# Sums of weight blocks by adding DMAs, with the products of neighbouring pairs interleaved

## The chip, the cores and the metric

The kernel runs on one core of one Trainium2 chip. The metric is the device time of one execution, in microseconds (us).

## What is computed

A decoder trunk of two layers on 512 positions of width 1024, batch 1, everything in fp32. A layer has three steps; each adds to x a gated function of a modulated RMS norm of x:

```python
x = x + 0.5 * gate[:, 0] * swiglu(ada(x, 0), ffn_w1[l, 0], ffn_w2[l, 0])
x = x + gate[:, 1] * mixer(ada(x, 1), w_in[l], ..., w_out[l])
x = x + 0.5 * gate[:, 2] * swiglu(ada(x, 2), ffn_w1[l, 1], ffn_w2[l, 1])
```

`ada(x, i)` is `rmsnorm(x) * (1 + scale_i) + shift_i`; shift, scale and gate are `silu(c) @ w_ada[l] + b_ada[l]`. `swiglu(h)` is `(silu(h @ w1_gate) * (h @ w1_up)) @ w2`, with a hidden width of 2816. The mixer is dilated attention beside a short convolution; the change does not touch it.

## The kernel before, in words

**Number format.** Every fp32 weight block and activation is split into two fp32r parts, hi (an ACT copy) and lo (a DVE subtraction); a product is three matmuls, hi*hi, hi*lo and lo*hi (`halves` L159, `product` L249, `shared_bulk` L255).

**FFN, first matrix.** The 22 hidden tiles of 128 are taken as 11 pairs. A pair's 1024 x 256 part of w1 (gate and up) is four blocks of 128 x 1024, b11, b12, b21 and b22, and the pair is computed with seven products of 2x2 blocks (Winograd's form of Strassen) in place of eight. Products 1, 2 and 4 take the loaded blocks b11, b12, b22. The others take sums of blocks: 5 takes s = b21 + b22, 6 takes s - b11, 7 takes b11 - b21 as combined at L199, 3 takes b12 - (s - b11). Before, all of them are loaded by SP (seven loads of 512 KB for a pair, `load_unit` L173), and DVE makes the four sums (`combine` L185 in `split_unit` L180). One product of a pair is called a unit here: 24 matmuls of 256 columns.

**FFN, second matrix.** After pairs 3, 7 and 10 the finished part of w2 is multiplied ("part" 0, 1, 2): eight steps of 128 output rows, for each a load of 512 or 384 KB, a split, and products over all 512 positions (`Tail.run` L477). Within a pair the products accumulate in three PSUM banks a, b, c of six (L596); `evacuation` (L549) copies bank a with ACT (L564) between the products that share it, adds on DVE (L559), and ends in `hidden` (L566), whose hi and lo parts are what the w2 products read.

**Order.** `_ffn_order` (L83) writes the order of the units out by hand. All weights go through one list of units; `weights` (L219) asks for splits two units ahead of the one in use (AHEAD), and `fetch` (L209) for loads two units ahead of those (LOADED). Loaded blocks lie in six tiles of tag "raw" (L151), the split ones in four tiles each of "whi" and "wlo" (L161). SP issues every load in order, and waits where the next tile is not free.

**Modulation jobs.** The weights w_ada of later steps are reduced by jobs put between the units (`later` L314, `next_job` L307): a job loads a 512 KB block into one of the same six "raw" tiles (`ada_load` L274) and reduces it on DVE (`ada_job` L278, L282). One job follows each pair, three each of the first four pairs of the first FFN (L636), and two each step of a w2 part (L509). The jobs of the second FFN of layer 1 are none: nothing comes after it.

**Ends of steps.** The last part of a step ends in the norm for the next (`Blocks` L423, `change` L526): its first half goes to a tile "hva" of its own, and the seven moving operands of the block products are made from it.

Of the kernel before, what the change touches and what calls it, by code (L numbers as in the profile page):

```python
# [18 lines left out]
D = 1024  # L19
# [83 lines left out]
def trunk(ctx: ExitStack, tc: tile.TileContext, t: dict):  # L103
# [47 lines left out]
    def raw_tile(name="raw"):  # L151
        return wp.tile([128, 1024], F32, name=name, tag="raw", bufs=6)
# [18 lines left out]
    blocks = {}  # L171

    def load_unit(key, src, n):  # L173

        if key[0] != "w1":
            return [load(src, n)]
        b11, b12, b21, b22 = (src[b] for b in range(4))
        return [load(b) for b in {1: (b11,), 2: (b12,), 3: (b12,), 4: (b22,), 5: (b21, b22), 6: (b11,), 7: ()}[key[4]]]

    def split_unit(key, raws, n):  # L180
        if key[0] == "w1":
            pair, which = key[:4], key[4]

            def combine(out, a, b, op):
                nc.vector.tensor_tensor(out=out, in0=a, in1=b, op=op)  # L185

            if which == 5:
                a21, s = raws
                combine(s, a21, s, ALU.add)
                blocks[pair] = [a21, s]  # L190
                raws = [s]
            elif which == 6:
                (a11,), (a21, s) = raws, blocks[pair]
                combine(s, s, a11, ALU.subtract)
                blocks[pair].append(a11)
                raws = [s]
            elif which == 7:
                a21, _, a11 = blocks[pair]
                combine(a11, a11, a21, ALU.subtract)  # L199
                raws = [a11]  # L200
            elif which == 3:
                (a12,), s = raws, blocks.pop(pair)[1]
                combine(a12, a12, s, ALU.subtract)
        return halves(key, raws[0], n)
# [4 lines left out]
    def fetch(upto):  # L209
        for i in range(len(loaded), min(upto + LOADED, len(order))):  # L210
            loaded.append(load_unit(*order[i]))
        for i in range(len(fetched), min(upto, len(order))):
            key, _, n = order[i]
            fetched.append(split_unit(key, loaded[i], n))
            loaded[i] = None
# [58 lines left out]
    def ada_load(w, l, s, m, j):  # L274
        nc.sync.dma_start(w, t["w_ada"][l, (s * 3 + m) * KD + j])
        return w

    def ada_job(l, s, m, j, w=None):  # L278
        raw, _ = mods[l, s]
        if w is None:  # L280
            w = ada_load(raw_tile("ada"), l, s, m, j)
        nc.vector.scalar_tensor_tensor(w, w, 1.0, cb, op0=ALU.mult, op1=ALU.mult,  # L282
                                       accum_out=raw[:, m, j:j + 1])
# [22 lines left out]

    def next_job(n=1):  # L307
# [115 lines left out]
    class Blocks:  # L423

        def __init__(self, l, s, h, pool):
            self.l, self.s, self.h, self.pool = l, s, h, pool

            self.first = [pool.tile([128, KD, 256], F32, name="hva", tag="hva", bufs=1)]

        def half(self, rb, which, k):  # L430

            l, s, h, cols = self.l, self.s, self.h, HALVES[which]
            first = self.first[0]
            a, b = 2 * k, 2 * k + 1
            if which == 0:
                for j, product in ((a, 1), (b, 2)):
                    scaled(first[:, j], l, s, rb, cols, j)
                    shifted(*moving(h, k, product), l, s, first[:, j], j)
# [7 lines left out]
            nc.vector.tensor_tensor(out=v[:, 0], in0=z[:, 0], in1=first[:, a], op=ALU.subtract)  # L446
# [4 lines left out]
            nc.vector.scalar_tensor_tensor(v[:, 3], first[:, b], shift, v[:, 2], op0=ALU.add, op1=ALU.subtract)  # L451
# [9 lines left out]
    class Tail:  # L461
# [15 lines left out]
        def run(self, ks, key, done, pool=None, side_by_side=0):  # L477
# [38 lines left out]
            if not self.last:  # L516
                h = new_h()
                blocks = Blocks(self.nl, self.ns, h, pool) if self.ns != 1 else None
# [97 lines left out]
    def ffn(l, s, h, carried, groups=()):  # L616
# [16 lines left out]
        for group in todo:  # L633
# [10 lines left out]
            room = None  # L644
            if p == len(PARTS) - 1 and s == 2 and l + 1 < DEPTH:
                room = stack.enter_context(tc.tile_pool(name="next", bufs=1))
# [5 lines left out]
    def mixer(l, s, h):  # L652
# [13 lines left out]
        with tc.tile_pool(name="mix", bufs=1) as mp:  # L666
# [142 lines left out]
            for i, k in enumerate((4, 5, 6, 7, 0, 1, 2, 3)):  # L809
                split(yh[i], yl[i], y[k])  # L810
                ks.append((yh[i], yl[i]))
        stack = ExitStack()
# [3 lines left out]
        return tail.run(ks, ("out", l), True, op), stack  # L816


    mod_tile(0, 0)
    stack = ExitStack()  # L820
# [7 lines left out]
    c = sp.tile([1, D], F32, name="c")  # L828
    nc.sync.dma_start(c, t["c"])
# [6 lines left out]
    for half in range(2):  # L836
        ps = acc_bank()
        cols = slice(half * 512, half * 512 + 512)
        nc.tensor.matmul(ps, row, c[:, cols], start=True, stop=True)
# [6 lines left out]
    first = Blocks(0, 0, h, sp)  # L846
    for k in range(KD // 2):
# [3 lines left out]
        for j in (2 * k, 2 * k + 1):  # L851
            for m in range(2):
                ada_job(0, 0, m, j, ada[j][:, m])
# [13 lines left out]
    for l in range(DEPTH):  # L867
        for s in range(3):
            if s == 1:
                stack.close()  # L870
                h, stack = mixer(l, s, h)
# [3 lines left out]
    stack.close()  # L875

# [62 lines left out]
```

## Time and profile before

| what | value |
|---|---|
| time, median of 3 runs | 1958.61 us (1956.05 to 1959.87) |
| time of the profiled execution | 1960.68 us |
| its span, first to last instruction | 1958.9 us |
| TensorE (PE) busy | 1856.1 us, 95% |
| VectorE (DVE) busy | 1551.4 us, 79% |
| ScalarE (ACT) busy | 898.7 us, 46% |
| GpSimd (POOL) busy | 11.9 us, 1% |
| mean granted TensorE clock, of full speed | 0.979 |
| bytes moved | 323.61 MB, 165 GB/s over the span |

The profile is one execution. An engine's busy time is the union of its instructions; matmuls are pipelined, so the time of one is longer than the step from one to the next. "Idle before" a group of instructions is the time in which their engine had nothing running just before them, put down to what ended it. The DMA share is the mean busy share of the core's 16 DMA engines.

### The profile page before, as it was taken

Reading aid. Unit: us, or ns where it says so; the run is one execution under the profiler, and the core shown is the slowest. Engines: PE = TensorE matmul, PEld = TensorE weight load, DVE = VectorE, ACT = ScalarE, POOL = GpSimd, SP = SyncE. Lnnn points to the kernel's source line nnn. Section 1 sums busy time; section 2 is a strip of 40 time slices with the busy share of each in tenths; the row PEclk is TensorE's granted clock in tenths of the full one; section 3 lists DMA queues with packets and bytes.
Section 4 is the critical chain, followed back from the end, with each engine's and each line's share of the span. In section 5 each row is a group of like instructions: output and inputs, shape, how many; then the busy total and the mean of one; then the engine's idle time right before and its main releaser. Section 6 shows DMA issues by size and latency. Waiting matters only on the chain.

```text
span 1958.9 us, 31198 instructions
## 1 busy us (share of the span) xinstructions
PE 1856.1 (95%) x12340; PEld 1718.4 (88%) x12340; DVE 1551.4 (79%) x2593; ACT 898.7 (46%) x1382; POOL 11.9 (1%) x76
## 2 busy tenths in 40 slices
PE   3899999999999899999989999999999998999999
PEld 2888998988988898998978989899898798989898
DVE  8987887897866998884779879788978669858574
ACT  3542442546654453452545425344656535535342
POOL 0000000000000000000000000000000000000000
PEclk9999999999999899999999999999999998999999
DMA  8478667642222167663524676766222123536442
GB/s 325 139 239 277 210 220 239 203 159 70 98 76 97 58 210 263 216 221 114 162 92 162 216 257 205 240 233 208 81 82 94 66 86 121 200 112 198 135 144 83
DMA packets 92613, 323.61 MB, mean 165 GB/s; under 512 B 10161, under 2 KB 11185, under 8 KB 92466
## 3 DMA queue, kind: packets, MB, share of 16 engines
q1 hardware_dynamic: 92466, 321.61, 49.0%
q8 instruction: 97, 1.59, 0.3%
q14 instruction: 50, 0.41, 0.1%
HBM read 319.48 MB, written 2.10 MB: 164 GB/s over the span
## 4 chain that ended last, share of the span: by engine, by line
PE 67%; DVE 17%; DMA 10%; issue 3%; ACT 3%; DVEq 0%; ACTq 0%
PE acc L258 31%; PE acc L251 11%; PE acc L252 10%; PE acc L253 10%; DMA ada<-in_w_ada 8%; DVE wlo L164 4%; DVE ada L282 4%; DVE raw L185 2%; ACT whi L163 2%; DMA raw<-in_w 2%; PE acc L739 1%; DVE h L458 1%; DVE ev L559 1%; PE tp L730 1%; PE tp L759 1%
## 5 line engine op out<-in xcount | busy, mean ns | idle before, releaser
L258 PE MATMUL acc<-h,whi 128*128 128x256 f32 x4928 | 905.6, 287 | 59.7 <-DVE ev L559 25.5
L258 PEld LDWEIGHTS acc<-h,whi 128*128 128x128 f32 x4928 | 776.8, 193 | 67.6 <-issue 26.0
L163 ACT ACTIVATE whi<-raw 128x1024 fp32r<-128x1024 f32 (+1 forms) x476 | 487.2, 1032 | 649.5 <-PE acc L252 298.0
L258 PE MATMUL acc<-h,wlo 128*128 128x256 f32 x2464 | 703.0, 286 | 11.4 <-DVE wlo L164 11.2
L164 DVE TENSOR_TENSOR wlo<-raw,whi 128x1024 fp32r<-128x1024 f32 (+1 forms) x476 | 562.4, 1187 | 90.1 <-ACT whi L163 85.2
L258 PEld LDWEIGHTS acc<-h,wlo 128*128 128x128 f32 x2464 | 475.3, 193 | 14.7 <-DVE wlo L164 14.5
L251 PE MATMUL acc<-hidh,whi 128*128 128x512 f32 (+1 forms) x776 | 286.9, 370 | 0.0
L253 PE MATMUL acc<-hidh,wlo 128*128 128x512 f32 (+1 forms) x776 | 286.7, 370 | 0.0
L252 PE MATMUL acc<-hidl,whi 128*128 128x512 f32 (+1 forms) x776 | 286.7, 369 | 0.0
L185 DVE TENSOR_TENSOR raw<-raw 128x1024 f32<-128x1024 f32 x176 | 214.5, 1221 | 33.6 <-DMA raw<-in_w 32.2
L282 DVE SCALAR_TENSOR_TENSOR ada<-ada,cb 128x1024 f32<-128x1024 f32 x144 | 175.3, 1223 | 59.8 <-DMA ada<-in_w_ada 53.4
L471 DVE SCALAR_TENSOR_TENSOR x<-acc,fin,x 128x512 f32<-128x512 f32 (+1 forms) x130 | 87.6, 675 | 112.1 <-PE acc L253 111.8
L253 PEld LDWEIGHTS acc<-hidh,wlo 128*128 128x128 f32 x776 | 146.3, 188 | 25.0 <-DVE wlo L164 0.2
L252 PEld LDWEIGHTS acc<-hidl,whi 128*128 128x128 f32 x776 | 146.3, 188 | 24.2
L251 PEld LDWEIGHTS acc<-hidh,whi 128*128 128x128 f32 x776 | 146.3, 189 | 24.1
L251 PE MATMUL acc<-h,whi 128*128 128x512 f32 (+1 forms) x368 | 139.8, 380 | 0.0
L252 PE MATMUL acc<-h,whi 128*128 128x512 f32 (+1 forms) x368 | 134.9, 367 | 0.0
L253 PE MATMUL acc<-h,wlo 128*128 128x512 f32 (+1 forms) x368 | 134.7, 366 | 0.0
L564 ACT ACTIVATE ev<-acc 128x512 f32<-128x512 f32 x132 | 76.6, 587 | 58.4 <-PE acc L258 58.4
L559 DVE TENSOR_TENSOR ev<-acc,ev 128x512 f32<-128x512 f32 x132 | 90.5, 687 | 9.5 <-PE acc L258 9.5
L251 PE MATMUL acc<-whi,h 128*128 128x384 f32 x256 | 90.1, 353 | 2.6 <-ACT h L414 2.6
L252 PE MATMUL acc<-wlo,h 128*128 128x384 f32 x256 | 88.0, 344 | 0.0
(99 smaller groups left out, 1669.1 us busy)
## 6 DMA issues: line engine op xcount, KB each, us to landing
raw<-in_w SPq DMA_DIRECT2D x308, 512.0 KB, 3.8
ada<-in_w_ada SPq DMA_DIRECT2D x128, 512.0 KB, 4.4
raw<-in_w2a SPq DMA_DIRECT2D x64, 512.0 KB, 4.2
raw<-in_w2b SPq DMA_DIRECT2D x32, 384.0 KB, 3.1
raw<-in_w_qkv SPq DMA_DIRECT2D x32, 384.0 KB, 3.5
raw<-in_w_gcu SPq DMA_DIRECT2D x24, 512.0 KB, 3.2
ada<-in_w_ada SPq DMA_DIRECT2D x8, 1024.0 KB, 7.3
raw<-in_w_out SPq DMA_DIRECT2D x16, 512.0 KB, 3.2
```

The source lines that it names most:

```text
L163: nc.scalar.activation(hi, raw, AF.Copy)
L164: nc.vector.tensor_tensor(out=lo, in0=raw, in1=hi.bitcast(F32), op=ALU.subtract)
L185: nc.vector.tensor_tensor(out=out, in0=a, in1=b, op=op)
L251: nc.tensor.matmul(out, a[0], b[0], start=first, stop=False)
L252: nc.tensor.matmul(out, a[0], b[1], start=False, stop=False)
L253: nc.tensor.matmul(out, a[1], b[0], start=False, stop=last)
L258: nc.tensor.matmul(out, p, q, start=first and i == 0, stop=i == 2, skip_group_check=True)
L282: nc.vector.scalar_tensor_tensor(w, w, 1.0, cb, op0=ALU.mult, op1=ALU.mult, accum_out=raw[:, m, j:j + 1])
L458: return nc.vector.tensor_tensor(out=lo, in0=v, in1=hi.bitcast(F32), op=ALU.subtract)
L471: nc.vector.scalar_tensor_tensor(x[j][:, cols], ps, gate, x[j][:, cols], op0=ALU.mult, op1=ALU.add)
L559: nc.vector.tensor_tensor(out=v, in0=bank, in1=v, op=ALU.add)
L564: nc.scalar.activation(sums_of[n, i], banks[n, "a"], AF.Copy)
```

## The change

SP loads only b11, b12, b22 and b21 for a pair. The sums are made by four transfers that POOL issues with an addition onto a tile in SBUF: b22 onto the loaded b21 (s); s, from SBUF, onto b11 after ACT has negated it in place (s - b11, in a new tag "sum" with three tiles); b22 onto a "raw" tile in which ACT has written the negated s - b11; b12 onto the negated s - b11. The four DVE sums of a pair go. `_ffn_order` gets a new order from pair 1 on. Job weights get two tiles of their own (tag "ada"), and their load is issued one job ahead and outside the `issue_after` that holds the job's work behind the last `hidden`. To make room, "hva" takes tiles of the tags "hidh" and "hidl" (or a pair of tiles in the pools of the start and of the mixer), c is loaded as two halves into working tiles, and the scratch of the DMAs that POOL issues is set to 4096 bytes.

```diff
@@ _ffn_order
-    order += [[u] for u in ((1, 5), (0, 7), (1, 6), (0, 4), (0, 3), (2, 5), (1, 7), (2, 6), (1, 4), (1, 3), (3, 1),
-                            (2, 7), (3, 5), (2, 4), (2, 3), (3, 6), (3, 2), (3, 7))]
+    order += [[u] for u in ((1, 5), (1, 6), (2, 5), (0, 7), (0, 4), (0, 3), (1, 7), (2, 6), (1, 4), (1, 3))]
     ends = [p0 + n - 1 for p0, n in PARTS]
-    for n in range(3, NP):
-        if n > 3:
-            order += [[(n, 5)], [(n, 6)]]
-            if n - 1 in ends:
-                order += [[("part", ends.index(n - 1))]]
-            order += [[(n, 2)], [(n, 7)]]
-        if n + 1 < NP:
-            order += [[(n + 1, 1)]]
-        order += [[(n, 4)], [(n, 3)]]
-    return order + [[("part", len(PARTS) - 1)]]
+    for n in range(3, NP + 1):
+        if n < NP:
+            order += [[(n, p)] for p in (1, 2, 5)]
+        order += [[(n - 1, 7)]]
+        if n < NP:
+            order += [[(n, 6)]]
+        order += [[(n - 1, p)] for p in (4, 3)]
+        if n - 1 in ends:
+            order += [[("part", ends.index(n - 1))]]
+    return order
@@ trunk
+    def negated(out, v):
+        nc.scalar.activation(out, v, AF.Copy, scale=-1.0)
+
+    def add_block(out, src):
+        nc.gpsimd.dma_start(out, src, accum_op=ALU.add)
+
     def load_unit(key, src, n):
...
+        pair, which = key[:4], key[4]
+        if which == 1:
+            a = sum_pool[0].tile([128, 1024], F32, name="sum", tag="sum", bufs=3)
+            nc.sync.dma_start(a, b11)
+            blocks[pair] = {"sum": a}
+            return a
+        if which in (2, 4):
+            return load(b12 if which == 2 else b22)
+        if which == 5:
+            s = load(b21)
+            add_block(s, b22)
+            blocks[pair]["lower"] = s
+            lower_added(pair)
+            return s
+        return None
+
+    def lower_added(pair):
+        b = blocks[pair]
+        if "negated" in b and "lower" in b:
+            add_block(b["sum"], b["lower"])
+
+    def split_unit(key, raw, src, n):
...
+        if which == 1:
+            out = halves(key, raw)
+            negated(raw, raw)
+            b["negated"] = True
+            lower_added(pair)
+            return out
+        if which == 6:
+            a = b["sum"]
+            out = halves(key, a)
+            b["third"] = raw_tile()
+            negated(b["third"], a)
+            add_block(b["third"], src[3])
+            negated(a, a)
+            add_block(a, src[1])
+            return out
+        if which == 7:
+            raw = b["third"]
+        elif which == 3:
+            raw = blocks.pop(pair)["sum"]
+        return halves(key, raw)
@@ jobs
+    def ada_load(l, s, m, j):
+        w = wp.tile([128, D], F32, name="ada", tag="ada", bufs=2)
         nc.sync.dma_start(w, t["w_ada"][l, (s * 3 + m) * KD + j])
         return w
...
         for _ in range(n):
             if jobs:
+                fetch_job(2)
                 f, args = jobs.pop(0)
+                w = ready.pop(0)
                 with tc.issue_after(ended[0].ins) if ended else nullcontext():
-                    f(*args)
+                    f(*w, *args)
+
+    def fetch_job(n):
+        for f, args in jobs[len(ready):n]:
+            ready.append([ada_load(*args)] if f is ada_job else [])
@@ kernel
-    nc = bacc.Bacc("TRN2", target_bir_lowering=False, num_devices=1)
+    nc = bacc.Bacc("TRN2", target_bir_lowering=False, num_devices=1, dynamic_dma_scratch_size=4096)
```

## Rows read from the trace of the kernel before

**Rows 1.** The page: busy time, share of the span and instructions of each engine.

```profile
PE 1856.1 (95%) x12340; PEld 1718.4 (88%) x12340; DVE 1551.4 (79%) x2593; ACT 898.7 (46%) x1382; POOL 11.9 (1%) x76
```

**Rows 2.** Windows by stage, L258 alone: between w2 parts 0 and 1 of each FFN.

```profile
core 0: us, PE busy (x) PEld busy (x), PEclk, DMA share, GB/s
194.54:280.26 85.72, 82.04 (x672) 81.79 (x671) 0.96 0.62 209
789.72:873.82 84.10, 81.30 (x672) 81.05 (x671) 0.98 0.61 208
1155.62:1242.46 86.84, 82.34 (x672) 82.09 (x671) 0.96 0.63 207
1747.58:1827.09 79.51, 79.51 (x672) 79.47 (x671) 1.00 0.53 173
```

**Rows 3.** The same view, L258 alone: between w2 parts 1 and 2 of each FFN.

```profile
323.80:373.40 49.60, 47.21 (x384) 46.96 (x383) 0.97 0.62 211
917.35:962.79 45.44, 45.44 (x384) 45.39 (x383) 1.00 0.48 157
1286.00:1333.04 47.04, 45.70 (x384) 45.45 (x383) 1.00 0.63 213
1870.66:1916.10 45.44, 45.44 (x384) 45.39 (x383) 1.00 0.49 157
```

**Rows 4.** Windows, all lines: the products of each FFN ahead of w2 part 0.

```profile
core 0: us, PE busy (x) PEld busy (x) DVE busy (x) ACT busy (x) POOL busy (x), PEclk, DMA share, GB/s
60.00:151.00 91.00, 84.12 (x668) 81.93 (x667) 83.77 (x102) 47.13 (x60) 0.00 (x0) 0.97 0.62 203
676.00:746.18 70.18, 68.95 (x577) 68.34 (x577) 64.76 (x71) 38.14 (x49) 0.00 (x0) 1.00 0.61 204
1040.00:1112.07 72.07, 70.46 (x586) 69.51 (x584) 65.01 (x72) 38.48 (x49) 0.00 (x0) 1.00 0.60 198
1633.00:1704.04 71.04, 70.68 (x596) 70.47 (x596) 65.60 (x70) 41.16 (x51) 0.00 (x0) 1.00 0.59 193
```

**Rows 5.** The chain that ended last, 1152 to 1169: start us, us, what.

```profile
1152.75 4.31 DMA ada<-in_w_ada
...
1158.30 0.10 DVE ada L282
1158.40 0.02 issue
1158.41 4.49 DMA raw<-in_w
...
1163.03 0.11 DVE raw L185
...
1168.26 0.49 ACT ev L564
```

**Rows 6.** Waits of PE from 60 us on: total us, times, longest us.

```profile
PE acc L258 <- DVE ev L559: 25.5, 3, 8.6
PE acc L258 <- ACT ev L564: 17.8, 8, 4.5
```

**Rows 7.** The page's costliest groups: busy us, mean ns, idle before us and what ended it.

```profile
L163 ACT ACTIVATE whi<-raw 128x1024 fp32r<-128x1024 f32 (+1 forms) x476 | 487.2, 1032 | 649.5 <-PE acc L252 298.0
L185 DVE TENSOR_TENSOR raw<-raw 128x1024 f32<-128x1024 f32 x176 | 214.5, 1221 | 33.6 <-DMA raw<-in_w 32.2
L282 DVE SCALAR_TENSOR_TENSOR ada<-ada,cb 128x1024 f32<-128x1024 f32 x144 | 175.3, 1223 | 59.8 <-DMA ada<-in_w_ada 53.4
```

**Rows 8.** Timeline of DVE at 1003 to 1006, ahead of the third FFN's first products.

```profile
1003.75 1.23 DVE L164 TENSOR_TENSOR wlo<-raw,whi 128x1024 fp32r<-128x1024 f32 x1
...
1005.30 1.22 DVE L185 TENSOR_TENSOR raw<-raw 128x1024 f32<-128x1024 f32 x1
1006.43 1.25 DVE L410 SCALAR_TENSOR_TENSOR hva<-x,fin,tp 128x256 f32<-128x256 f32 x3
```

**Rows 9.** The page's DMA issues (KB each, us to landing), and a window of queued loads.

```profile
raw<-in_w SPq DMA_DIRECT2D x308, 512.0 KB, 3.8
...
10.00:20.00 10.00, 1.87 (x8) 1.78 (x8) 7.60 (x21) 6.68 (x10) 0.00 (x0) 1.00 1.04 403
```

**Rows 10.** A w2 part (window), and DVE's timeline from the last unit before another.

```profile
280.26:323.80 43.54, 43.54 (x194) 36.05 (x193) 31.07 (x47) 9.03 (x10) 0.00 (x0) 1.00 0.79 264
...
1340.54 0.69 DVE L559 TENSOR_TENSOR ev<-acc,ev 128x512 f32<-128x512 f32 x1 [0.47 <-PE acc L258]
...
1343.62 0.69 DVE L458 TENSOR_TENSOR hidl<-hid,hidh 128x512 fp32r<-128x512 f32 x1 [0.70 <-ACT hidh L457]
```

More of the change, by code (lines that the diff above doesn't have):

```diff
@@ L171, in trunk @@
     blocks = {}
+    sum_pool = []
+    def negated(out, v):
+        nc.scalar.activation(out, v, AF.Copy, scale=-1.0)
+    def add_block(out, src):
+        nc.gpsimd.dma_start(out, src, accum_op=ALU.add)
     def load_unit(key, src, n):
         if key[0] != "w1":
-            return [load(src, n)]
+            return load(src, n)
         b11, b12, b21, b22 = (src[b] for b in range(4))
-        return [load(b) for b in {1: (b11,), 2: (b12,), 3: (b12,), 4: (b22,), 5: (b21, b22), 6: (b11,), 7: ()}[key[4]]]
@@ L180, in split_unit @@
[L180 to L204, printed above, removed]
+        pair, which = key[:4], key[4]
@@ new lines, in split_unit @@
+    def split_unit(key, raw, src, n):
+        if key[0] != "w1":
+            return halves(key, raw, n)
+        pair, which = key[:4], key[4]
+        b = blocks[pair]
+        if which == 1:
[18 more added lines that the diff above has]
+        return halves(key, raw)
@@ L212, in fetch @@
         for i in range(len(fetched), min(upto, len(order))):
-            key, _, n = order[i]
-            fetched.append(split_unit(key, loaded[i], n))
+            key, src, n = order[i]
+            fetched.append(split_unit(key, loaded[i], src, n))
             loaded[i] = None
@@ L423, in trunk, with __init__ @@
     class Blocks:
-        def __init__(self, l, s, h, pool):
+        def __init__(self, l, s, h, pool, first):
             self.l, self.s, self.h, self.pool = l, s, h, pool
-            self.first = [pool.tile([128, KD, 256], F32, name="hva", tag="hva", bufs=1)]
+            self.first = [v[:, j * 256:j * 256 + 256] for v in first for j in range(KD // 2)]
         def half(self, rb, which, k):
             l, s, h, cols = self.l, self.s, self.h, HALVES[which]
-            first = self.first[0]
+            first = self.first
             a, b = 2 * k, 2 * k + 1
@@ L436, in half @@
                 for j, product in ((a, 1), (b, 2)):
[L437 to L438 removed]
+                    scaled(first[j], l, s, rb, cols, j)
+                    shifted(*moving(h, k, product), l, s, first[j], j)
                 return
@@ L643, in ffn, with room @@
             ks = [[z[:, f] for z in hid[n]] for n in range(p0, p0 + np) for f in range(2)]
-            room = None
-            if p == len(PARTS) - 1 and s == 2 and l + 1 < DEPTH:
-                room = stack.enter_context(tc.tile_pool(name="next", bufs=1))
+            def room():
+                hp = pool[0]
+                return (stack.enter_context(tc.tile_pool(name="next", bufs=1)),
+                        [hp.tile([128, D], F32, name="hva", tag=m, bufs=PARTS[0][1]) for m in ("hidh", "hidl")])
             out = tail.run(ks, ("w2", l, which, p), p == len(PARTS) - 1, room, 2 if p == len(PARTS) - 1 else 0)
@@ L815, in mixer, with first_tiles, open_sums @@
             place["out", l, j] = op, SPLIT
-        return tail.run(ks, ("out", l), True, op), stack
+        return tail.run(ks, ("out", l), True, lambda: (op, first_tiles(op))), stack
+    def first_tiles(pool):
+        return [pool.tile([128, D], F32, name="hva", tag="hva", bufs=2) for _ in range(2)]
+    def open_sums():
+        sum_stack.append(ExitStack())
+        sum_pool[:] = [sum_stack[0].enter_context(tc.tile_pool(name="sum", bufs=1))]
+    sum_stack = []
     mod_tile(0, 0)
+    open_sums()
     stack = ExitStack()
@@ L826, in load_ada @@
         nc.sync.dma_start(ada[-1], t["w_ada"][0, 0:2 * KD].rearrange("(m j) p n -> j p m n", m=2)[len(ada) - 1])
-    c = sp.tile([1, D], F32, name="c")
-    nc.sync.dma_start(c, t["c"])
+    c = [half_kb("c")[0:1] for _ in range(2)]
+    for half in range(2):
+        nc.sync.dma_start(c[half], t["c"][:, half * 512:half * 512 + 512])
     load_ada()
@@ L838, in trunk @@
         cols = slice(half * 512, half * 512 + 512)
-        nc.tensor.matmul(ps, row, c[:, cols], start=True, stop=True)
+        nc.tensor.matmul(ps, row, c[half], start=True, stop=True)
         nc.scalar.activation(cb[:, cols], ps, AF.Silu)
```

23 lines of the change are left out of this document (12 added, 11 removed).

## The prediction

> **What bounds the kernel now.** I began with the page: PE is busy 95% of the span, DVE 79%, ACT 46%, POOL 1% [rows 1]. PE is the bound, so only time in which PE waits, or runs at the lower of its clocks, can be won. Next I cut the trace into stages with like work, since the same products recur in all four FFNs. Between w2 parts 0 and 1 stand 672 matmuls each time: 79.51 us in the last FFN, at full clock and without a gap, but 85.72, 84.10 and 86.84 us in the other three [rows 2]. Between parts 1 and 2, 384 matmuls take 45.44 us twice, and 49.60 and 47.04 us [rows 3]. The undisturbed pace is 45.44 / 384 = 0.1183 us, so a unit of 24 is 2.84 us and a pair of 168 is 19.9 us. The last FFN makes all the DVE sums too, but has no modulation jobs: the sums alone do not hold PE up.
>
> What does is seen in the chain after a w2 part [rows 5]: a job's load (4.31 us), the job on DVE, which frees its "raw" tile, then the load of a w1 block that waited for that tile (4.49 us), then the sum, and only behind it ACT's copy of a bank for which PE stands. Eight such stands cost PE 17.8 us [rows 6]. The larger wait of PE, 25.5 us in three, is for DVE at the start of an FFN, where the norm's second half fills DVE.
>
> **The change, part by part.** The sum is made against the profiled execution: 1960.7 us, of which its span is 1958.9; the median of the runs, 1958.6, is 2.1 lower.
>
> *Stretches after a w2 part.* Against 79.5 and 45.4 us, [rows 2] hold 6.2 + 4.6 + 7.3 and [rows 3] 4.2 + 0 + 1.6 us, 23.9 together, stall and clock loss alike (the clock is granted at 0.96 to 0.98 of full there, at 1.00 in the last FFN). The change takes both links out of that chain: jobs no longer hold "raw" tiles and are loaded a job ahead, so that DVE loses its idle time before them (53.4 us, [rows 7]), and no DVE sum stands before the bank adds. I take 22 as won; the ends are 0 and 24.
>
> *First stretches.* At the same pace the 668, 577, 586 and 596 matmuls of [rows 4] should take 79.0, 68.3, 69.3 and 70.5 us; they take 12.0, 1.9, 2.7 and 0.5 more. In the first FFN, with three jobs a pair, DVE works 83.77 us for 668 / 168 = 3.98 pairs, 21.1 us a pair, more than PE's 19.9. The four sums removed are 4 x 1.22 = 4.9 us a pair [rows 7], which leaves 16.2. Of these 17.1 us I take 9 as won, since the first pairs are also where the DMA engines fill up (below); the ends are 0 and 15.
>
> *Between the second and the third FFN* a sum and a split stand on DVE just before the norm's first half [rows 8], with PE soon to wait for it. Sum and knock-on: 3 us won, of 0 to 5. The 8.6 us waits behind the second half stay: DVE's work there is not touched.
>
> *The adding transfers.* No row shows one. The nearest is a plain load of 512 KB: 403 GB/s when queued, so 524 kB / 403 = 1.30 us of the engines, and 3.8 us from issue to landing [rows 9]. One that adds must also fetch what it adds to. The lower end is a plain load (1.30); the upper is two reads and a write, each as a transfer of its own (3.9, and 11.4 us to land). I take two, 2.6 us, as the source and the old contents are both read, and 3.8 + 1.3, with some queueing about 6 us, to land. The Trainium skill (Collectives: The Full Stack, "The bandwidth ceiling: the fold count and why AG ≠ RS ≠ AR") says that an add in the DMA engines costs no time of its own but needs two source reads on the same ring, which halves the rate; the estimate by it is also 2.6 us, and no run here shows it yet.
>
> A pair then puts four plain and four adding loads on the engines: (4 + 4 x 2) x 0.524 = 6.3 MB-equivalents in 19.9 us, 316 GB/s against 403; with one job 342, with three jobs 395. That fits, barely in the first pairs, and costs 0 elsewhere. If the cover fails, see the first rival. SP issues three loads fewer a pair (308 become 176); the jobs' loads, moved ahead, are as many as before, and one waits only for the job two before it, which has long run when the next weights are behind it in SP's queue. POOL gets 176 transfers on an almost empty queue [rows 1]; they run in order, and an add that waits holds the next pair's behind it.
>
> *ACT.* Three negations of 1.03 us a pair [rows 7], 132 x 1.03 = 136 us in all. ACT works 41.16 us of 71.04 in [rows 4], so a pair's 3.1 us raise it from 58% to some 74%: hidden. But a negation waits for DVE's split of the same block, and the split of product 6 waits for an adding transfer, with the bank copies queued behind both on ACT. At the four FFN starts, where DVE is late, and in the start of the kernel, where loads already queue at 1.04 of the engines [rows 9], I put 3 us lost, of 0 to 8.
>
> *Entry into w2 parts 0 and 1.* The new order puts the part right behind product 3 of its last pair; before, two units lay between. From the end of that product to the last hidden split are 1343.62 + 0.69 - 1340.54 = 3.8 us on idle queues [rows 10]. A part has 192 matmuls in 43.5 us, 0.227 each [rows 10], and six of its eight K tiles come first: 6 x 3 x 0.227 = 4.1 us of cover. One split in the way on DVE or ACT breaks it: 0 to 2 us at each of 8 entries, I take 5 in all, of 0 to 16. Part 2 was entered this way before and did not stop.
>
> *Bank order.* The new order leaves more units between copies and reuse of bank a (five from product 6 to 7, before one); counted in the first term. The hva tiles, the halves of c and the small scratch: nothing, they are off PE's path.
>
> Sum: -22 - 9 - 3 + 3 + 5 = -26, so 1934.7; less 2.1, **1932.6 against a median of 1958.6** (-1.3%).
>
> **Rivals.**
>
> *The adding transfers set the pace (slower).* A pair's adds form a chain: b22 onto b21, that onto the negated block, then split and two negations before the last two adds: two round trips R and some 5 us (a split of 1.03 and 1.22, two negations, POOL's issues). It decides from 2 R + 5 > 19.9, R over 7.4 us. The splits are three units, 8.5 us, ahead, refilled in each w2 part, so four pairs can bear 2.1 us each: it costs from R = 8.5 on. At R = 9.5 a pair is 24, so 4.1 x 4 - 8.5 = 7.9 for each group of four and 3.8 for the three: 19.6 an FFN, 78 in all, about 2011. For it: the upper end of 11.4 us, and that two reads would bring the engines near their rate. Against it: 5 to 6 us by my own price. By the Trainium skill (DMA: Bandwidth & Descriptors, "Anatomy of one DMA — SWDGE (gpsimd) path") a POOL transfer takes about 2.0 us plus its bytes at 436 GB/s; the estimate is 4.4 us for twice 512 KB, below the deciding point; no run here shows it. A milder form, a few adds late in the first FFN where 395 of 403 GB/s are asked, gives 1965 to 1990. Chance of both together 0.25, the stronger 0.15.
>
> *The stalls only move (no change).* The jobs' loads, the adds and the w2 blocks still meet at the end of each part, half of the 22 stays, and the entries cost their upper 16: -11 - 3 - 3 + 3 + 16 = +2, about 1960. For it: all three meet where the DMA share is already 0.79 [rows 10]. Against: jobs and blocks have separate tiles. Chance 0.10.
>
> *All stretches reach the last FFN's pace,* and the entries are covered: -24 - 15 - 5 = -44, 1914 on the median's footing. For it: [rows 2] show the pace is possible. Against: the first pairs' DMA demand. Chance 0.15.
>
> **How the numbers follow.** A measurement of this kernel can tell about 0.2%, 3.9 us, from no change. The forecast (1920 to 1950) has 0.50; with the last rival 0.65 for faster. No change 0.10, slower 0.25. The range from 1912 to 1990 takes in all but the stronger form of the first rival and a little below; faster cases alone would span 1912 to 1950.
>
> **What would show it.** Right: in each of the four FFNs 672 matmuls in 80 us after part 0; no DVE line for the sums; DVE under 70%, ACT near 53% of the span; the jobs' idle time on DVE gone; adds landing within 7 us; PE still waiting some 8.6 us at three FFN starts. Wrong: PE waits put down to ACT's split or DVE's split behind an adding transfer, a DMA share near 1 through whole w1 stretches, POOL idle for transfers at 8.5 us or more, or new gaps at the first hidden operands of a w2 part.

## The result, and the profile after

The changed kernel takes 1975.15 us (median of 5 runs, 1974.9 to 1984.0) beside 1959.87 us of the kernel before on the same chip (5 runs, 1956.05 to 1961.43): a ratio of 1.009, 95% interval 1.0066 to 1.0114. It is slower, where I had forecast 1932.6 and a gain. The profiled execution spans 1973.1 us, 14.2 more than before.

The page of the changed kernel, its span and busy time:

```profile
span 1973.1 us, 31443 instructions
PE 1860.2 (94%) x12340; PEld 1718.9 (87%) x12340; DVE 1358.5 (69%) x2417; ACT 1017.1 (52%) x1514; POOL 164.5 (8%) x252
```

The work moved as the edit says: DVE fell to 69%, ACT rose to 52%, POOL now issues transfers [rows 1]. PE gained nothing.

Windows by stage show where the 14.2 us are. Columns as in [rows 4]. Before, the first FFN (first to last product of w1) and the two stages from the last w1 product of an FFN over the mixer to the first product of the next FFN:

```profile
23.20:380.60 357.40, 326.91 (x2238) 306.77 (x2239) 308.57 (x409) 148.15 (x184) 0.00 (x0) 0.97 0.67 224
380.60:644.20 263.60, 258.33 (x1486) 229.95 (x1485) 203.64 (x556) 139.90 (x303) 5.81 (x36) 0.99 0.31 101
...
1340.20:1603.50 263.30, 257.92 (x1485) 229.74 (x1484) 202.70 (x554) 139.93 (x303) 5.87 (x36) 0.99 0.30 100
```

And the changed kernel, the same three stages:

```profile
23.40:377.30 353.90, 321.90 (x2237) 302.03 (x2238) 258.70 (x364) 175.62 (x216) 38.28 (x44) 0.96 0.87 245
377.30:650.80 273.50, 262.02 (x1485) 233.44 (x1484) 202.39 (x555) 143.46 (x307) 11.91 (x43) 0.97 0.36 110
...
1345.90:1616.90 271.00, 260.44 (x1485) 232.03 (x1484) 201.49 (x553) 143.53 (x307) 11.90 (x43) 0.97 0.36 105
```

The four FFNs together are 4.6 us shorter (-3.5, -0.1, -1.6, +0.6), and the boundary between the second and the third is 0.8 longer. The two mixer stages, in which not one product was changed, are 9.9 and 7.7 us longer. That is more than the whole loss.

One execution of each kernel is compared here. In the other kernels of this study that lack the long wait described below, the first mixer stage lasts 264.5 to 268.1 us and the second 262.2 to 265.9, so the 263.6 before lies low and the two losses are sure to a few us only. In the two stages PE stands 6.2 and 5.2 us longer than before; the rest is longer busy time, at a granted clock of 0.97 beside 0.99.

Between w2 parts 0 and 1, the w1 products alone (L285; the rows that answer to [rows 2]), and the first of those between parts 1 and 2 [rows 3], which now hold 360 matmuls, 42.6 us at full pace. (The windows of [rows 3] and these end two units before part 2: 432 matmuls lie between parts 1 and 2 before, 408 now. The loss does not change by it.)

```profile
200.02:281.76 81.74, 80.05 (x672) 79.59 (x671) 1.00 0.92 247
799.17:882.67 83.50, 81.27 (x672) 81.02 (x671) 0.98 0.93 248
1168.47:1250.50 82.03, 80.05 (x672) 79.59 (x671) 1.00 0.94 252
1763.94:1843.46 79.52, 79.52 (x672) 79.47 (x671) 1.00 0.80 201
...
325.63:370.00 44.37, 43.13 (x360) 42.68 (x359) 1.00 0.78 204
```

Against 79.5 the first four lose 2.2 + 4.0 + 2.5 + 0 us, and the stretches between parts 1 and 2 another 3.4 (44.37, 42.60, 44.23, 42.60): 12.1 in all, where before lost 23.9. So the stretches did gain, 11.8 us and not 22. The DMA share of 0.92 to 0.94, 0.62 before, is the first new thing in these rows.

More stands in the waits of the changed kernel (engine, tile and line, what it waited for: total us, times, longest us):

```profile
ACT raw L174 <- DMA sum<-raw: 145.3, 41, 8.1
...
PE tp L418 <- DVE ssq L410: 25.2, 8, 10.8
PE acc L285 <- ACT h L449: 23.4, 6, 12.2
DVE ada L308 <- DMA ada<-in_w_ada: 79.4, 62, 3.6
```

L174 with the output "raw" is the negation that writes the third tile of a pair, minus (s - b11). It needs the end of the adding transfer sum<-raw, and in 41 of the 44 pairs ACT stood for it, 145.3 us. ACT is far from being the bound, so most of this is free. It isn't free where something that PE needs soon is queued behind it on ACT. The first such place, on ACT's timeline (start us, us, engine, line, operation; idle before and what ended it):

```profile
52.48 1.06 ACT L492 ACTIVATE h<-hvb 128x1024 fp32r<-128x1024 f32 x1 [1.41 <-DVE hvb L486]
61.66 1.06 ACT L174 ACTIVATE raw<-sum 128x1024 f32<-128x1024 f32 x1 [8.12 <-DMA sum<-raw]
64.44 1.06 ACT L174 ACTIVATE raw<-sum 128x1024 f32<-128x1024 f32 x1 [1.72 <-DMA sum<-raw]
65.40 0.89 ACT L449 ACTIVATE h<-hva,fin 128x256 fp32r<-128x256 f32 x2
...
636.99 1.06 ACT L174 ACTIVATE raw<-sum 128x1024 f32<-128x1024 f32 x1 [7.07 <-DMA sum<-raw]
637.95 0.40 ACT L409 ACTIVATE sq<-x 128x256 f32<-128x256 f32 x1
```

At 52.5 us ACT stops for two adding transfers, and the moving operands h that PE waits for come at 65.4: this is PE's longest wait there, 12.2 us. Before, ACT wrote these operands at 58.0 us, and PE's longest wait for h was 4.7. At 630 us, the end of the first mixer, ACT stops again, and the squares of the norm stand behind it. DVE shows the next link, the sum of the squares:

```profile
638.38 0.42 DVE L410 TENSOR_TENSOR ssq<-ssq,sq 128x256 f32<-128x256 f32 x1 [6.73 <-ACT sq L409]
```

and PE stands from 636 us for 5.0 us at L418, the row sums of the norm; at the end of the second mixer it stands 4.6 us there, before 1.0 at both. No weight block is late here. A first pair's weights are being prepared early, as they should be, and the preparation blocks the engine that finishes the step before.

In the stretches the wait is another one, on DVE. Some 10 us after a w2 part PE stands for the lo part of a w1 block. The hi copy of the block, then DVE, then PE in the second FFN:

```profile
799.14 1.06 ACT L162 ACTIVATE whi<-raw 128x1024 fp32r<-128x1024 f32 x1 [0.47 <-PE acc L279]
...
807.23 1.23 DVE L308 SCALAR_TENSOR_TENSOR ada<-ada,cb 128x1024 f32<-128x1024 f32 x1 [3.60 <-DMA ada<-in_w_ada]
809.04 1.22 DVE L163 TENSOR_TENSOR wlo<-raw,whi 128x1024 fp32r<-128x1024 f32 x1
...
810.32 0.58 PE L285 MATMUL acc<-h,wlo 128*128 128x256 f32 x1 [2.23 <-DVE wlo L163]
```

The hi copy is done at 800.2 us, but the lo split stands on DVE behind two modulation jobs that wait for their weights, 1.0 and 3.6 us. The same stands in all five stretches that lose time: DVE waits 2.9 to 4.6 us for two jobs' loads, and PE then 0.7 to 2.2 us for the lo part. (In the kernel with plain transfers below, DVE waits 1.8 to 2.9 us at the three places after part 0, and PE not at all.) These are 6.7 of the 8.2 us that PE stands in the five. All jobs' waits on DVE rose from 53.4 [rows 7] to 79.4 us; the stretches of the last FFN, which has no jobs, lose nothing. This is read from the trace; no run tested it by moving the jobs.

The page's DMA queues (packets, MB, share of the 16 engines) and issues (KB each, median us to landing) of the changed kernel:

```profile
q1 hardware_dynamic: 73460, 252.40, 36.5%
q0 software_dynamic: 25344, 92.29, 26.2%
...
raw<-in_w POOLq DMA_DIRECT2D x88, 512.0 KB, 6.5
...
sum<-raw POOLq DMA_DIRECT2D x44, 512.0 KB, 5.3
sum<-in_w POOLq DMA_DIRECT2D x44, 512.0 KB, 7.5
```

An adding transfer took 0.262 x 1973.1 / 176 = 2.94 us of the engines, and landed after 5.3 to 7.5 us. A load by SP took 0.365 x 1973.1 us for 252.40 MB, which is 1.50 us for 512 KB.

### The profile page after: what moved, and what is told of

Same layout as the page of the kernel before. It is cut to its first block, busy times and chain, and to the rows that moved or that the text cites. A ratio compares the mean times of both kernels' runs of the same rounds, so it can differ in the third digit from the quotient of the medians.

```text
span 1973.1 us, 31443 instructions
## 1 busy us (share of the span) xinstructions
PE 1860.2 (94%) x12340; PEld 1718.9 (87%) x12340; DVE 1358.5 (69%) x2417; ACT 1017.1 (52%) x1514; POOL 164.5 (8%) x252
## 3 DMA queue, kind: packets, MB, share of 16 engines
q1 hardware_dynamic: 73460, 252.40, 36.5%
## 5 line engine op out<-in xcount | busy, mean ns | idle before, releaser
L285 PE MATMUL acc<-h,whi 128*128 128x256 f32 x4928 | 901.0, 286 | 53.5 <-ACT h L449 23.4
L285 PEld LDWEIGHTS acc<-h,whi 128*128 128x128 f32 x4928 | 773.5, 193 | 61.5 <-ACT h L449 25.2
L285 PE MATMUL acc<-h,wlo 128*128 128x256 f32 x2464 | 700.8, 285 | 14.7 <-DVE wlo L163 14.7
L163 DVE TENSOR_TENSOR wlo<-raw,whi 128x1024 fp32r<-128x1024 f32 (+1 forms) x344 | 402.9, 1173 | 182.2 <-ACT whi L162 178.1
L162 ACT ACTIVATE whi<-raw 128x1024 fp32r<-128x1024 f32 (+1 forms) x344 | 348.2, 1016 | 326.2 <-PE acc L279 177.2
L285 PEld LDWEIGHTS acc<-h,wlo 128*128 128x128 f32 x2464 | 473.0, 192 | 17.7 <-DVE wlo L163 17.7
L308 DVE SCALAR_TENSOR_TENSOR ada<-ada,cb 128x1024 f32<-128x1024 f32 x144 | 174.8, 1224 | 85.5 <-DMA ada<-in_w_ada 79.4
L163 DVE TENSOR_TENSOR wlo<-sum,whi 128x1024 fp32r<-128x1024 f32 x132 | 160.6, 1223 | 66.1 <-ACT whi L162 65.1
L162 ACT ACTIVATE whi<-sum 128x1024 fp32r<-128x1024 f32 x132 | 138.6, 1055 | 120.8 <-PE acc L285 74.0
L174 ACT ACTIVATE sum<-sum 128x1024 f32<-128x1024 f32 x88 | 93.3, 1060 | 100.3 <-DVE wlo L163 100.0
L177 POOL DMA_DIRECT2D raw<-in_w x88 | 76.5, 893 | 664.9 <-ACT raw L174 240.2
L174 ACT ACTIVATE raw<-sum 128x1024 f32<-128x1024 f32 x44 | 46.6, 1059 | 145.3 <-DMA sum<-raw 145.3
```

The source lines that it names most:

```text
L162: nc.scalar.activation(hi, raw, AF.Copy)
L163: nc.vector.tensor_tensor(out=lo, in0=raw, in1=hi.bitcast(F32), op=ALU.subtract)
L174: nc.scalar.activation(out, v, AF.Copy, scale=-1.0)
L177: nc.gpsimd.dma_start(out, src, accum_op=ALU.add)
L285: nc.tensor.matmul(out, p, q, start=first and i == 0, stop=i == 2, skip_group_check=True)
```

## The experiments

Each kernel below was timed against the kernel before on the same chip. Ratios are to that, so that runs of different chips can stand side by side; the kernel before had medians of 1959.87 to 1963.65 us there.

The expectations speak of theories, and the letters change. In the first ones (the jobs' tiles, the negation behind for all pairs, the negations on POOL, the old order) theory A is that ACT waits in order for an adding transfer, and theory B that the DMA engines are too full. In the kernels with some transfers plain it is the other way round: A is the load of the engines, B the length of what is waited for. Where they give an adding transfer 3.9 us of the engines, the upper end in the prediction, the trace of the changed kernel gives 2.94.

**The jobs' tiles alone.** The order and the DVE sums of before, six "raw" tiles; only the jobs get their own two tiles, with the load one job ahead and outside the `issue_after`. The room made for them (hva, c, the small scratch) is as in the changed kernel.

```diff
-            w = ada_load(raw_tile("ada"), l, s, m, j)
+        w = wp.tile([128, D], F32, name="ada", tag="ada", bufs=2)
+        nc.sync.dma_start(w, t["w_ada"][l, (s * 3 + m) * KD + j])
...
+                fetch_job(2)
```

> The modulation jobs' own two tiles and their loads a job ahead alone: sums on DVE from seven loads, and the order of the products, as before. If the jobs' tiles made the stalls after the w2 parts, 672 matmuls take 79.5 to 81.5 us in all four FFNs and the time falls by 12 to 24 us, 1935 to 1947, with no adding transfer anywhere. If those stalls need DVE free of the sums, it stays within 5 us of before, 1953 to 1963. Theories A and B both say that it has none of the losses at the start and at the mixers' ends.

Measured: 1939.94 us, ratio 0.9884 (0.9838 to 0.9929). Windows of this kernel between parts 0 and 1, and the jobs' wait on DVE:

```profile
193.17:272.68 79.51, 79.51 (x672) 79.47 (x671) 1.00 0.64 214
786.00:865.52 79.52, 79.52 (x672) 79.47 (x671) 1.00 0.62 209
1146.96:1226.48 79.52, 79.52 (x672) 79.47 (x671) 1.00 0.65 215
1732.25:1811.77 79.52, 79.52 (x672) 79.47 (x671) 1.00 0.53 173
```

```profile
DVE ada L282 <- DMA ada<-in_w_ada: 52.5, 57, 5.9
```

All four stretches run at the pace of the last FFN (and all four between parts 1 and 2 in 45.44 us). The time lies in the range of the first expectation. So the chain of [rows 5] was read rightly, and the change to the jobs alone cuts it. The jobs still stand for their loads on DVE, 52.5 us beside 53.4 before [rows 7]; what has gone is that a job in waiting holds a tile that a w1 block needs. (Tiles of their own and the earlier load were not tried one without the other.) A seventh "raw" tile in the same kernel:

```diff
-        return wp.tile([128, 1024], F32, name=name, tag="raw", bufs=6)
+        return wp.tile([128, 1024], F32, name=name, tag="raw", bufs=7)
```

> The jobs' own tiles alone, with seven raw tiles instead of six: loads of the first FFN's products run further ahead. The stretches are at full pace already; between 60 and 150 us some 12 us are lost beside full speed. If loads are short there, 3 to 8 us less than 1940; if DVE is (21 us of work for a pair of 19.9), no change: 1936 to 1944.

Measured: 1933.85 us, ratio 0.987 (0.9851 to 0.9889). This is the fastest kernel of this study that computes everything; its interval overlaps that with six tiles, so the seventh tile's own gain is not shown. Between parts 0 and 1 this kernel's four stretches took 80.5, 81.6, 79.6 and 79.5 us, so the jobs' own tiles do not give the full pace every time.

**The adding transfers made plain.** Same instructions in the same order on every engine as in the changed kernel; only the addition in POOL's transfers is left out, and with it the four sums.

```diff
-        nc.gpsimd.dma_start(out, src, accum_op=ALU.add)
+        nc.gpsimd.dma_start(out, src)
```

> The change with POOL's 176 transfers plain instead of adding; the sums are left out (products 5, 6, 7 and 3 take the block that is copied last), while waits, tiles and the order are those of the change. Theory A1, the length of the round trips: a plain transfer needs about 1.5 us of the DMA engines in place of some 3.9, the round trips shrink from 5 to 8 us to 4 or 5, ACT waits less for them, and the time is 1945 to 1962. Theory A2, the number of hand-overs (POOL, semaphores, ACT's negations in order), whatever a transfer takes: 1965 to 1978.

Measured: 1931.07 us, ratio 0.985 (0.9832 to 0.9868), 44 us below the changed kernel and below both expected ranges. The page's DMA rows, a wait and two windows of this kernel:

```profile
q0 software_dynamic: 25344, 92.29, 13.3%
...
raw<-in_w POOLq DMA_DIRECT2D x88, 512.0 KB, 4.9
...
sum<-raw POOLq DMA_DIRECT2D x44, 512.0 KB, 3.1
sum<-in_w POOLq DMA_DIRECT2D x44, 512.0 KB, 4.3
```

```profile
ACT raw L174 <- DMA sum<-raw: 50.4, 20, 5.7
```

```profile
23.70:364.80 341.10, 318.19 (x2237) 299.36 (x2238) 259.50 (x364) 177.16 (x216) 23.35 (x44) 0.97 0.72 254
364.80:631.20 266.40, 258.06 (x1486) 230.04 (x1486) 203.02 (x555) 143.10 (x307) 9.50 (x43) 0.99 0.34 113
```

A plain transfer takes 0.133 x 1929.8 / 176 = 1.46 us of the engines, so the addition costs 2.94 / 1.46 = 2.0 times as much, and 1.6 to 3.2 us more to land. ACT's stand falls from 145.3 to 50.4 us. The first FFN is 12.8 us shorter than in the changed kernel, the mixer stages 7.1 and 6.4, the other FFNs 5.6, 9.4 and 0.7, the boundary 1.7. Between parts 0 and 1 all four stretches take 79.5 us at a DMA share of 0.57 to 0.73. So it is the additions that make the change slow. Negations, new order and new tiles together, with transfers that cost no more than loads, would have given the 1932.6 that I had forecast. That agreement says little for my sum, since the jobs' tiles alone come within 1 to 7 us of it.

**Which of the four additions.** Two kernels, again with the changed kernel's instructions in the same order on every engine. In the first only b22 onto b21 and s onto the negated b11 add (the chain for whose end ACT waits), and the last two transfers are plain; in the second it is the other way round. The sums of the plain ones are left out.

```diff
-            add_block(b["third"], src[3])
+            nc.gpsimd.dma_start(b["third"], src[3])
...
-            add_block(a, src[1])
+            nc.gpsimd.dma_start(a, src[1])
```

> Of the four transfers that POOL issues for a pair only the first two add (b22 onto b21, and that onto the negated b11: the chain for whose end ACT waits in order); the last two (b22 onto the third tile, b12 onto the negated sum) are plain, so that their two sums are left out. Every engine has its instructions in the same order as in the changed kernel. With all four adding the time is 1975 us, with all four plain 1931. Theory A, what costs is the load of the adding transfers on the engines, whichever they are: half of the 44 us comes back, 1946 to 1960 us, and the same with the other two adding. Theory B, what costs is the length of the chain that ACT waits for: 1962 to 1977 us here.

> The complement: the first two transfers of a pair are plain (their sums are left out), the last two add. Same order of the instructions on every engine. Theory A, load: 1946 to 1960 us. Theory B, the chain: 1929 to 1943 us.

Measured: 1968.48 us, ratio 1.0031 (1.001 to 1.0051), with the chain adding; 1944.41 us, ratio 0.9914 (0.9883 to 0.9944), with the last two. From 0.985 with none, the chain adds 1.8 points and the last two 0.6, together what all four add (1.009 - 0.985 = 2.4). Both kinds put nearly the same load on the engines (POOL's queue has 20.4% and 20.1% of them), so load alone, theory A, would have made the two equal. Theory B holds for the chain; with the last two adding, the time is 1.4 us above its range, so these cost something as well. Where each costs is seen by stage. The first mixer stage, with the chain adding and then with the last two adding:

```profile
380.30:649.70 269.40, 257.03 (x1486) 228.70 (x1484) 202.47 (x555) 143.28 (x307) 11.31 (x43) 0.99 0.36 112
...
371.10:635.60 264.50, 256.92 (x1486) 228.34 (x1485) 202.50 (x555) 143.50 (x307) 10.28 (x43) 0.99 0.36 114
```

The second mixer stage took 272.2 and 265.9 us. At the row sums that end the two stages PE stands 4.5 and 5.8 us with the chain adding, 0.6 and 1.3 with the last two. So in the mixer stages the chain's additions cost, and the last two hardly do. In the stretches both cost, 7.9 and 5.5 us over the four between parts 0 and 1; with the last two adding, DVE stands for two jobs' loads in the first, 1.6 and 3.5 us, ahead of the lo part for which PE waits 1.9. ACT's waits, first with the chain adding:

```profile
ACT raw L174 <- DMA sum<-raw: 135.8, 41, 8.9
```

then with the last two adding:

```profile
ACT raw L174 <- DMA sum<-raw: 69.3, 28, 7.4
```

**ACT's order, in the first pairs.** The negation into the third tile is put behind the hi copy of product 6 on ACT, for pairs 0 and 1 of each FFN: these are prepared while the step before ends.

```diff
-            negated(b["third"], a)
+            with tc.issue_after(copies[-1].ins) if pair[3] < 2 else nullcontext():
+                negated(b["third"], a)
```

> The change with the negated third tile queued behind the hi copy of product 6 on ACT, for pairs 0 and 1 of each FFN alone, those whose sums fall beside the norm. The run with it for every pair got the start and the mixers' ends back, but lost more in the stretches between the w2 parts. Theory A, two places with one cause (ACT waits in order for a round trip: at the norm it delays the squares, in the stretches it delays the bank copies or the next add): the start and both mixers' ends come out as in the kernel before and the stretches as in the change, 1945 to 1962. If the time is 1970 or more, the loss at the ends is not from this negation.

Measured: 1957.27 us, ratio 0.9969 (0.9948 to 0.999), 18 us below the changed kernel, with all its additions, and within the expected range. The two mixer stages of this kernel:

```profile
378.80:646.10 267.30, 259.50 (x1486) 231.08 (x1485) 202.96 (x555) 141.84 (x305) 9.29 (x40) 0.98 0.34 107
1337.10:1599.30 262.20, 256.70 (x1486) 228.17 (x1485) 201.69 (x553) 141.75 (x305) 9.29 (x40) 0.99 0.33 103
```

They are 6.2 and 8.8 us shorter than in the changed kernel, 15 of the 18. The loss of the mixer stages is thus ACT's wait in order, and not the transfers as such. At the start of the first FFN the edit removes the wait of 12.2 us as well (the longest for h is now 4.8), but PE then waits 6.4 us for ACT's hi copies, and the time to part 0 is only about 1 us shorter.

The same for all pairs (the condition on the pair is left out):

> The change with one edit: ACT writes the negated third tile (the target of the add of b22) only after it has issued the hi copy of product 6; nothing else moves by hand. Theory A, ACT's order: in the changed kernel this negation stood ahead of the norm's squares and operand copies in ACT's queue, and waited 7 to 12 us for an adding transfer at the start and at the end of both mixers. Then those waits go: 12.4 us at 53 us, 5 to 8 us at each mixer's end, 2 to 5 us between the second and third FFN, some 20 to 28 us in all, so 1947 to 1957. Theory B, the DMA engines are too full with adds at 3.9 us each: the order on ACT does not matter, 1970 to 1980.

Measured: 2017.92 us, ratio 1.0279 (1.0237 to 1.0321), above both expected ranges; the expected gain did not come. The mixer stages recovered here too (265.6 and 263.9 us), but the stretches are lost. A window of this kernel between parts 0 and 1, and its largest wait of PE:

```profile
203.05:296.07 93.02, 84.78 (x672) 82.92 (x671) 0.96 0.79 210
```

```profile
PE acc L287 <- ACT ev L601: 46.3, 21, 5.2
```

Within the stretches the negation has to run early, since two more transfers hang on it: POOL's wait for it rises from 240.2 to 426.5 us. So neither of the two settings serves both places. The build also moved much else on ACT in this kernel, so it shows that the edit costs, and not each link of how.

**Negations on POOL.**

```diff
-        nc.scalar.activation(out, v, AF.Copy, scale=-1.0)
+        nc.gpsimd.tensor_scalar(out, v, -1.0, None, op0=ALU.mult)
```

> The change with all three negations of a pair on POOL in place of ACT. Theory A: ACT no longer waits for adding transfers except in the hi copy of product 6, so the start and the mixers' ends lose nothing and the time is 1945 to 1960, unless POOL's own negations (unknown, 1 to 2.5 us each, three a pair) make the chain of adds too long; then PE shows waits for the hi or lo of products 6, 7 and 3 inside the long stretches. Theory B: 1970 to 1985, as the transfers are the same.

Measured: 1976.61 us, ratio 1.0089 (1.0057 to 1.0122). That is in the range of theory B, but not for its reason: the mixer stages recovered (264.8 and 264.1), as theory A had it, and each negation takes three times ACT's 1.06 us and delays the transfers behind it on POOL. The group of the two in-place ones of a pair's negations on POOL (busy us, mean ns, idle before), and PE's largest wait:

```profile
L174 POOL TENSOR_SCALAR sum<-sum 128x1024 f32<-128x1024 f32 x88 | 268.5, 3051 | 373.3 <-DVE wlo L163 367.2 <-issue 4.1 <-DMA raw<-in_w 2.0
```

```profile
PE acc L285 <- ACT ev L599: 32.3, 22, 3.5
```

PE's 32.3 us for bank copies were 11.1 in the changed kernel.

**The order of products.** Additions and jobs' tiles as in the changed kernel, with `_ffn_order` of before:

> The change with the order of the products as before (adding transfers and jobs ahead kept). Theory A: the losses at the start and at the mixers' ends hang on ACT's queue and not on the order of pairs, so they stay, and the time is 1968 to 1990. Theory C, the new order itself loses (entries into the w2 parts, the first products): 1950 to 1965.

Measured: 2059.77 us, ratio 1.0495 (1.0439 to 1.0551), outside both ranges. A window of this kernel between parts 0 and 1 (PE alone), and its largest wait of PE:

```profile
199.10:308.40 109.30, 88.02 (x673) 0.88 0.75 193
```

```profile
PE acc L286 <- ACT ev L600: 93.2, 31, 11.6
```

In the old order products 5, 6 and 7 of a pair follow closely, and two transfers must land between them. The new order is what makes the additions bearable: it is worth some 80 us here (1.0495 - 1.009 of 1961). Conversely the new order and the jobs' tiles with the sums on DVE (s in one of the "sum" tiles):

> The new order and the jobs' own tiles, with the sums on DVE as before (s lies in the three sum tiles): against the run with the jobs' tiles alone (1940) only the order differs. The stretches were already at full pace there, so the order has nothing to win: 1935 to 1948. If the entries into w2 parts 0 and 1 right behind product 3 cost what I put on them (5 us, up to 16), 1944 to 1956.

Measured: 1951.95 us, ratio 0.9953 (0.9934 to 0.9971). The time lies in the second range, where entries into w2 parts had been expected to cost, but they are not the cause: a part lasts 43.8 us as in the changed kernel. The first two windows of this kernel between parts 0 and 1:

```profile
192.70:274.71 82.01, 80.57 (x672) 79.70 (x671) 1.00 0.64 216
784.70:868.57 83.87, 80.84 (x672) 79.79 (x671) 1.00 0.62 211
```

It loses 10.7 us over the four of these and 4.6 between parts 1 and 2. With plain transfers the same order loses nothing there. In each of the first three DVE's sums stand 9 to 11 us for loads of w1 blocks, and PE waits for a lo part and for a bank copy, up to 2.0 us; why these loads come late in this order stays open.

**Load without length.** Two kernels tried to part the engines' load from the length of a transfer: plain transfers (sums left out), and for each a second one from DRAM to a DRAM block that nothing reads, once behind and once ahead of the awaited one.

```diff
-        nc.gpsimd.dma_start(out, src, accum_op=ALU.add)
+        nc.gpsimd.dma_start(out, src)
+        more(block)
```

> The transfers that POOL issues are plain, as in the run that gave 1931 us, and the sums are left out; behind each of them POOL issues a second plain transfer of 512 KB from DRAM to a DRAM block that nothing reads. So the engines get about the load of the adding transfers (26% of the span on POOL's queue, against 13% without), but the transfer that ACT and DVE wait for stays a short one. Theory A, the engines' load is what costs (other loads and the later sums queue behind it): 1962 to 1985 us, close to the changed kernel's 1975. Theory B, the awaited round trip itself is what costs, in the places where ACT or DVE waits for it in order: 1928 to 1945 us.

> As the run before it, but the second plain transfer is issued ahead of the awaited one, which so lands about one transfer later (some 1.3 to 3 us), with the same load. Theory A, load alone: the same time as with the second one behind, within 5 us. Theory B, the round trip: 1955 to 1985 us, at least 15 us above the run with the second one behind.

Measured: 2189.84 us, ratio 1.1169 (1.1138 to 1.1201), and 2194.64 us, ratio 1.1184 (1.1156 to 1.1213), far outside both theories. Nothing follows for the question: with more transfers in the program the build put the instructions of every engine in another order, the negations and the split copies on ACT among them, and PE then waits most for ACT's hi copies (119.6 us with the second transfer behind). This is why the two kernels above change only the kind of a transfer and leave the order as it is.

## Why the prediction was wrong

The span grew by 14.2 us where my sum had -26. By its steps:

| step | predicted, us | measured, us |
|---|---|---|
| stretches after a w2 part | -22 (-24 to 0) | -11.8 |
| first stretches, from the first product to part 0 | -9 (-15 to 0) | +4.1 |
| boundary of second and third FFN | -3 (-5 to 0) | +0.8 |
| adding transfers | 0 | in the other rows; +44 beside the kernel with plain ones |
| negations on ACT, at FFN starts and kernel start | +3 (0 to 8) | in the rows above and below |
| entries into parts 0 and 1 | +5 (0 to 16) | +2.5 |
| mixer stages | none | +17.6 |

The measured terms are differences of windows; the first stretches last 450.3 us for 4 x 768 matmuls, before 434.9 for 4 x 744, which at 0.1183 us leaves 86.9 beside 82.8. They sum to 13.2 of the 14.2.

*What was right.* The chain in [rows 5] and the size of what it costs: the kernel with the jobs' tiles alone is 21.7 us faster, and its stretches lose nothing. The price of an adding transfer, 2.6 us of the engines and about 6 to land, came out at 2.94 and 5.3 to 7.5. The entries and their cover. DVE at 69% and ACT at 52% of the span. Not so the sign that the jobs' idle time on DVE would be gone: it rose from 53.4 to 79.4 us.

*The step that failed* is the one that set the adding transfers at no cost outside the first pairs, because eight blocks' worth of bandwidth fitted into a pair's 19.9 us. Beside plain transfers they cost 44 us, more than the 40 by which the sum was off. Two things were wrong in the step.

First, the fit was tighter than the sum had it. At the measured 2.94 us for an adding transfer and 1.50 for a load, a pair asks 4 x 2.94 + 4 x 1.50 = 17.8 us of the engines, 19.3 with one job and 22.3 with three; this is an estimate from the rows above. The sum had 0.78, 0.85 and 0.98 of what the engines give; these are 0.89, 0.97 and 1.12. So in the first FFN's first pairs it did not fit at all.

Second, the sum asked only whether the bytes fit, and not which engine with other work waits in order for a landing. I had written that a negation waits, with bank copies queued behind it on ACT, and then put 3 us on it, at the FFN starts and the kernel's start only. The first pair's transfers run while the step before ends, and behind the same negation stood the squares of the norm and the moving operands. The end of the mixer was not among my places at all, and its two stages are 17.6 us longer, of which 15 come back when the negation is moved. In the stretches, where the sum had 22 us won and 11.8 came, it was DVE that stood behind the jobs' late loads, as the trace shows.

*The rival that was nearest* had the adding transfers set the pace, with a deciding round trip of 7.4 us and costs from 8.5. The sign and the range of its milder form (1965 to 1990) were right, and with three jobs a pair the engines were asked for more than they give, where it had 395 of 403 GB/s. But the loss was not a few late adds in the first FFN alone. Transfers that land in 5.3 us (sum<-raw), well below the deciding point, already cost: PE pays for single waits of ACT (7 to 8 us) and of DVE (up to 3.6 us) at places where its next operands are queued behind them. My rule for the DMA share was also too lenient: 0.92 to 0.94 in the first three stretches after part 0, which I had counted as fitting, goes with a loss of 8.7 us, and without the additions, at 0.70 to 0.73, there is none.

The Trainium skill (Collectives: The Full Stack, "The bandwidth ceiling: the fold count and why AG ≠ RS ≠ AR") says of ring collectives that a reducing transfer needs two source reads and so runs at half the rate; the 2.94 beside 1.46 us agree, factor 2.0, for an addition onto SBUF. The estimate by the Trainium skill (DMA: Bandwidth & Descriptors, "Anatomy of one DMA — SWDGE (gpsimd) path"), 2.0 us plus bytes at 436 GB/s, is 3.2 us for a plain 512 KB; the median of the plain sum<-raw is 3.1, those from DRAM took 4.3 to 4.9 beside the other loads; the 4.4 us for twice the bytes is below all that the adding ones took.

*What stays open.* How much of the first stretches' loss is load and how much is length was not parted. That the jobs' loads come late because of the load on the engines is argued from the stretches (shares of 0.92 to 0.94 beside 0.70 to 0.73), and not tested apart. The additions with the negation in another place for each pair, worked out by hand, were not tried beyond the two settings above.

## What to carry to other kernels

When work is moved from an engine into a transfer, don't only ask whether the bandwidth is there. List every instruction that waits for the transfer's landing, on which in-order engine it stands, and what is queued behind it at every place where it runs, the ends of unrelated steps included. And cost the parts of a combined change apart: here one part (tiles of their own for the jobs' weights) holds the whole gain, 1.2 to 1.3%, and the other gives it back and more.

## What the runs showed that was not expected

An addition onto SBUF doubles a 512 KB transfer's time on the engines (1.46 to 2.94 us) and adds 1.6 to 3.2 us to its landing under this load. Putting the negation of just two pairs of eleven further back on ACT changed the time by 18 us, and for all eleven by 43 us in the other direction. Jobs that stand 52.5 us for their loads on DVE cost PE nothing in the stretches, once they hold no tile that others need (DMA share up to 0.65); where they stand 79.4 us, under the additions, PE pays for it.
